# Stick-breaking attention with queries on partitions, VectorE's scan for the running product and weights turned by TensorE

## The chip, the core and the metric

The kernel runs on one core of a Trainium2 chip. The time is device microseconds of one execution. The median of three runs before is 2308.95 us (2308.16 to 2309.34). The profile is one such execution, taken with the hardware profiler.

## What is computed

A trunk of four residual layers (512 tokens, width 1024), each a token mixer and a dense SwiGLU FFN, in float32. Only layer 2 has the mixer that the change touches, stick-breaking attention with 16 heads of 64. Cut to what matters:

```python
def stick_breaking_mixer(h, w_qkv, q_norm, k_norm, w_out):
    qkv = (h @ w_qkv).reshape(b, s, 3, SB_HEADS, SB_HEAD_DIM)
    q, k = rms_norm(qkv[:, :, 0], q_norm), rms_norm(qkv[:, :, 1], k_norm)
    ...
    z = einsum('bhqd,bhkd->bhqk', q_blk, k) * inv_sqrt_d
    mask = key_pos[None, :] < t[:, None]
    log_1m = where(mask, log_sigmoid(-z), 0.0)
    after = cumsum(log_1m, axis=3, reverse=True) - log_1m
    a = where(mask, exp(log_sigmoid(z) + after), 0.0)
    o = einsum('bhqk,bhkd->bhqd', a, v)
    ...
    return o @ w_out
```

A weight is the sigmoid of its own z times the product of the sigmoids of -z of all later keys in front of the query.

## The kernel before

Activations lie as features x tokens. Each big product is made of three of rounded halves (high x high, high x low, low x high): `gemm`, lines 215 to 217. The weights come by SyncE's DMA queue; ScalarE rounds a piece (`wh`, line 108) and VectorE takes the rest (`wl`, line 109), up to four pieces ahead. A scheduler arranges the instructions of each engine when the program is built; which step comes first in the source is set by the string `ATT_STEPS`, and the weights are loaded in the same order.

The steps of the attention are: `pair` (p0 to p7), the projections of q and k for two heads, their normalization (`normal`, with Square, a sum by TensorE, Ln, Exp and Square on ScalarE) and the halves `qq`, `ql`, `kk`; `values` (v0 to v3), v for four heads; `attend` (a0 to a7), two heads; `out` (o0 to o3), the output projection for four heads.

In an `attend` each head has keys on partitions: a tile of z for a block of 128 keys has the queries along the free dimension. Three PSUM tiles hold the causal part of a head, 256, 512 and 512 wide (`z2`, `z13`, `z0`), with a constant -2^100 added to what is masked (`never`, line 867). `softplus` makes log(1 + exp(z)) by Abs, Exp and Ln on ScalarE (lines 873 to 875) and a maximum and sum on VectorE (877); `halves` cuts the result into two rounded parts (881, 882). Since keys lie on partitions, the sum over later keys is a product with a triangle or with a matrix of -1 (`nger`, `none`; `add`, line 910), added into the same PSUM tile as z. An Exp (914) gives the weights, which have the layout that the product with v (842) needs. `split` (220, 221) cuts the output into halves for the output projection.

Of the kernel before, what the change touches and what calls it, by code (L numbers as in the profile page):

```python
# [36 lines left out]
HD = 64  # L37
# [90 lines left out]
def _steps(order, **names):  # L128
    return [(names[s[0]], int(s[1:])) for s in order.split()]
# [7 lines left out]
)  # L137

ATT_STEPS = _steps(
    "p0 v0 p1 a0 p2 v1 p3 a1 a2 p4 v2 o0 a3 p5 a4 v3 p6 o1 a5 p7 a6 a7 o2 o3",  # L140
    p="pair", v="values", a="attend", o="out",
)

SSD_BUFS = dict(u=2, state=3, f=11, a=6, w=6, o=8, c=2, d=5, sel=1)
ATT_BUFS = dict(kk=4, qq=4, ql=4, p=2, v=8, w=3, e=2, a=6, h=6, h2=2, l2=1, o=4)


class Trunk:
# [593 lines left out]
    def attention(self, j, nxt):  # L742
        nc = self.nc
        mm = nc.tensor.matmul
        V = nc.vector
        with self.phase("att", **ATT_BUFS) as tl:
            nge = self.t((P, P))
            nc.gpsimd.memset(nge, -1.0)
            nc.gpsimd.affine_select(
                out=nge, in_=nge, pattern=[[-1, P]], base=0, channel_multiplier=1,  # L750
                compare_op=ALU.is_ge, fill=0.0,
            )
            nger = tl("nger", (P, P), F32R)
            V.tensor_copy(nger, nge)
            none = tl("none", (P, P), F32R)
            V.tensor_scalar(none, self.ones, -1.0, None, op0=ALU.mult)
            V.memset(nge, 0.0)
            V.memset(nge[:HD, :HD], 1.0)
            V.memset(nge[HD:, HD:], 1.0)
            bd = tl("bd", (P, P), F32R)  # L760
            V.tensor_copy(bd, nge)
            qg = tl("qg", (P, 1))
            V.tensor_scalar(qg, self.col("q_norm", 0), 1.0 / math.sqrt(HD), None, op0=ALU.mult)
            kg = self.col("k_norm", 0)
            identb = tl("identb", (P, P), BF16)
            V.tensor_copy(identb, self.ident)
            nc.gpsimd.memset(nge, 0.0)
            nc.gpsimd.affine_select(
                out=nge, in_=nge, pattern=[[1, P]], base=0, channel_multiplier=-1,
                compare_op=ALU.is_gt, fill=-(2.0**100),  # L770
            )
            never = tl("never", (P, P), BF16)
            V.tensor_copy(never, nge)
            rcol = tl("rcol", (P, NB))

            turns = itertools.cycle("mymynmy")

            def bank(shape=(P, SEQ)):
                return self.ps(next(turns), shape)

            def project(q):
                ps = self.ps("g")
# [47 lines left out]
                    heads.append((qq, ql, kk))  # L830
                return heads

            def attend(f, heads, vt):
                po, av = self.ps("s"), []
                for h in range(2):
                    av.append(head(heads[h]))


                at = [(0, 0, 2), (0, 2, 4), (1, 2, 4), (2, 2, 4), (1, 1, 2), (3, 3, 4)]
                for i, (kb, lo, hi) in enumerate(at):  # L840
                    for h in range(2):
                        mm(  # L842
                            po[h * HD : (h + 1) * HD, lo * P : hi * P],
                            vt[kb][:, (2 * f + h) * HD : (2 * f + h + 1) * HD],
                            av[h][kb][:, (lo - kb) * P : (hi - kb) * P],
                            start=i == 0, stop=i == len(at) - 1,
                        )
# [4 lines left out]
            def head(parts):  # L852


                qq, ql, kk = parts

                def zmm(out, *kbs):


                    at = 0  # L860
                    for kb in kbs:
                        n = SEQ - kb * P
                        for i, q in enumerate((qq, ql)):
                            mm(out[:, at : at + n], kk[:, kb * P : (kb + 1) * P],  # L864
                               q[:, kb * P :], start=at == 0 and i == 0, stop=False)
                        at += n
                        mm(out[:, at - n : at - n + P], identb, never, start=False,
                           stop=kb == kbs[-1])

                def softplus(pz):  # L870
                    shape = pz.shape
                    e = tl("e", shape)
                    nc.scalar.activation(e, pz, AF.Abs)
                    nc.scalar.activation(e, e, AF.Exp, scale=-1.0)
                    nc.scalar.activation(e, e, AF.Ln, bias=1.0)
                    w = tl("w", shape)
                    V.scalar_tensor_tensor(w, pz, 0.0, e, op0=ALU.max, op1=ALU.add)
                    return w

                def halves(w, hi, lo):  # L880
                    V.tensor_copy(hi, w)
                    V.tensor_tensor(lo, w, hi.bitcast(F32), op=ALU.subtract)

                def flat(t):
                    return t.rearrange("p b t -> p (b t)")

                z2 = bank((P, 256))
                zmm(z2, 2)  # L890
                w2 = softplus(z2)


                h2, l2 = (tl(t, (P, 3, P), F32R) for t in ("h2", "l2"))
                halves(w2, flat(h2[:, :2]), flat(l2[:, :2]))
                z13 = bank()
                zmm(z13, 1, 3)
                w13 = softplus(z13)
                h13, l13 = tl("h", dt=F32R), tl("h", dt=F32R)
                halves(w13, h13, l13)  # L900
                V.tensor_tensor(w2[:, P:], w2[:, P:], w13[:, 384:], op=ALU.add)
                halves(w2[:, P:], h2[:, 2], l2[:, 2])
                z0 = bank()
                zmm(z0, 0)
                w0 = softplus(z0)
                h0, l0 = tl("h", dt=F32R), tl("h", dt=F32R)
                halves(w0, h0, l0)

                def add(out, left, right, last=False):
                    mm(out, left, right, start=False, stop=last, skip_group_check=True)  # L910

                def weights(z):
                    a = tl("a", z.shape)
                    nc.scalar.activation(a, z, AF.Exp)
                    return a

                both = slice(0, 3, 2)
                add(z2, nger, h2[:, :2])
                add(z2, nger, l2[:, :2])
                add(z2[:, P:], none, h13[:, 384:])  # L920
                add(z2[:, P:], none, l13[:, 384:], True)
                a2 = weights(z2)
                add(z13, nger, h13)
                add(z13, nger, l13)
                add(z13[:, P:384], none, h2[:, both])
                add(z13[:, P:384], none, l2[:, both], True)
                a13 = weights(z13)
                add(z0, nger, h0)
                add(z0, nger, l0)
                for p13, p2 in ((h13, h2), (l13, l2)):  # L930
                    add(z0[:, P:], none, p13[:, :384])
                    add(z0[:, 256:], none, p2[:, both], p2 is l2)
                a0 = weights(z0)
                return a0, a13[:, :384], a2, a13[:, 384:]

            def rstd_columns():

# [201 lines left out]
```

## Time and profile before

| what | us |
|---|---|
| median of three runs | 2308.95 |
| the profiled execution, whole | 2308.4 |
| its span, first to last instruction | 2306.5 |
| attention, first projection to a7's last product with v (1230.9 to 1518.7) | 287.8 |
| PE busy in the whole span | 2284.8 |
| VectorE busy | 1361.4 |
| ScalarE busy | 991.1 |

A matmul's busy time in this profile overlaps that of the next, so a row's mean duration of 0.39 us for a 512 wide matmul is not the time from its start to the start of the next one. The table has the engines' busy time; which wait ends last in a stretch is read from the stretch itself.

### The profile page before, as it was taken

To read this page: it belongs to the slowest core of one execution; us is meant where nothing else is said; L and a number is where in the kernel's file an instruction comes from. 1 tells how busy PE (TensorE), PEld (TensorE's weight loads), DVE (VectorE), ACT (ScalarE), POOL (GpSimd) and SP (SyncE) were. 2 spreads that over 40 slices of the span, in tenths; PEclk is the share of its full clock that TensorE was granted. 3 is DMA by queue.
4 is the path that set the end of the run, shared out by engine and by line. 5 is a ranking of instruction groups with operands and counts; after the bars stand their busy time and mean duration, and the time that the engine had idled before them with its cause. 6 is when DMAs were issued, how large, how long until landed. Compare 5 with 4: busy or idle time off the path is not lost.

```text
span 2306.5 us, 26600 instructions
## 1 busy us (share of the span) xinstructions
PE 2284.8 (99%) x10714; PEld 1857.9 (81%) x10714; DVE 1361.4 (59%) x1946; ACT 991.1 (43%) x1478; POOL 39.7 (2%) x134
## 2 busy tenths in 40 slices
PE   8999999999999999999999999999999999999999
PEld 6788888777877778888888787678888888888887
DVE  9743434778787785444346777874344469534443
ACT  5522323577565764222235766762222244322221
POOL 0000000000000000000000100100000000000000
PEclk9999999999999999999999999999999999999999
DMA  5323322322223222332223221122322223332231
GB/s 161 116 91 100 101 92 76 110 73 74 73 74 92 73 73 92 97 104 91 92 82 101 65 65 55 37 74 95 107 91 92 96 92 95 104 108 92 91 100 64
DMA packets 211898, 205.43 MB, mean 89 GB/s; under 512 B 4800, under 2 KB 204608, under 8 KB 211776
## 3 DMA queue, kind: packets, MB, share of 16 engines
q1 hardware_dynamic: 211632, 203.57, 27.7%
q8 instruction: 84, 1.38, 0.2%
q14 instruction: 38, 0.31, 0.0%
q10 hardware_dynamic: 144, 0.17, 0.0%
HBM read 201.63 MB, written 2.10 MB: 88 GB/s over the span
## 4 chain that ended last, share of the span: by engine, by line
PE 91%; DVE 4%; ACT 3%; DMA 1%; issue 1%; DVEq 0%; ACTq 0%
PE ps L215 28%; PE ps L217 27%; PE ps L216 27%; PE ps L910 2%; PE ps L842 1%; PE ps L673 1%; PE ps L864 1%; PE ps L679 1%; DMA raw<-in_pool_in_dram 1%; ACT wh L108 1%; DVE wl L109 1%; PE ps L642 0%; PE ps L805 0%; PE ps L806 0%; PE ps L804 0%
## 5 line engine op out<-in xcount | busy, mean ns | idle before, releaser
L108 ACT CAST wh<-raw 128x1024 fp32r<-128x1024 f32 (+3 forms) x394 | 402.8, 1023 | 1077.0 <-PE ps L216 838.6
L215 PE MATMUL ps<-xh,wh 128*128 128x512 f32 x2056 | 803.9, 392 | 6.4 <-ACT xh L261 5.9
L217 PE MATMUL ps<-xh,wl 128*128 128x512 f32 x2056 | 803.1, 391 | 0.3 <-DVE wl L109 0.3
L216 PE MATMUL ps<-xl,wh 128*128 128x512 f32 x2056 | 803.0, 391 | 0.3 <-DVE xl L262 0.3
L109 DVE TENSOR_TENSOR wl<-raw,wh 128x1024 fp32r<-128x1024 f32 (+3 forms) x394 | 467.9, 1188 | 77.9 <-ACT wh L108 77.3
L215 PEld LDWEIGHTS ps<-xh,wh 128*128 128x128 f32 x2056 | 385.8, 188 | 89.3 <-ACT xh L261 6.2
L217 PEld LDWEIGHTS ps<-xh,wl 128*128 128x128 f32 x2056 | 385.7, 188 | 83.0 <-issue 2.7
L216 PEld LDWEIGHTS ps<-xl,wh 128*128 128x128 f32 x2056 | 385.7, 188 | 82.0 <-DVE xl L262 1.9
L215 PE MATMUL ps<-h,wh 128*128 128x512 f32 x736 | 286.4, 389 | 0.9 <-DVE x L393 0.9
L216 PE MATMUL ps<-h,wh 128*128 128x512 f32 x736 | 286.3, 389 | 0.0
L217 PE MATMUL ps<-h,wl 128*128 128x512 f32 x736 | 286.3, 389 | 0.0
L343 DVE TENSOR_TENSOR x<-ps,x 128x512 f32<-128x512 f32 x96 | 66.4, 692 | 257.2 <-PE ps L217 257.2
L336 DVE TENSOR_TENSOR g<-ps,g 128x512 f32<-128x512 f32 x88 | 60.6, 691 | 226.3 <-PE ps L217 226.3
L327 DVE TENSOR_TENSOR g<-ps,rstd 128x512 f32<-128x512 f32 x88 | 60.6, 691 | 220.6 <-PE ps L217 220.5
L215 PEld LDWEIGHTS ps<-h,wh 128*128 128x128 f32 x736 | 138.2, 188 | 29.7 <-DVE x L393 1.3
L216 PEld LDWEIGHTS ps<-h,wh 128*128 128x128 f32 x736 | 138.2, 188 | 28.8
L217 PEld LDWEIGHTS ps<-h,wl 128*128 128x128 f32 x736 | 138.2, 188 | 28.8
L215 PE MATMUL ps<-o,wh 128*128 128x512 f32 x192 | 77.2, 405 | 1.2 <-DVE x L736 1.1
L216 PE MATMUL ps<-o,wh 128*128 128x512 f32 x192 | 77.5, 404 | 0.0
L217 PE MATMUL ps<-o,wl 128*128 128x512 f32 x192 | 76.6, 400 | 0.0
L457 DVE SCALAR_TENSOR_TENSOR c<-u,par,c 128x512 f32<-128x512 f32 x96 | 72.0, 750 | 4.1 <-ACT c L452 3.2
L330 DVE TENSOR_TENSOR g<-g,rstd 128x512 f32<-128x512 f32 x88 | 59.9, 685 | 2.6 <-ACT g L329 2.5
(199 smaller groups left out, 2114.0 us busy)
## 6 DMA issues: line engine op xcount, KB each, us to landing
raw<-in_ffn_gate_dram SPq DMA_DIRECT2D x44, 1024.0 KB, 5.1
raw<-in_ffn_up_dram SPq DMA_DIRECT2D x44, 1024.0 KB, 5.2
raw<-in_ffn_down_dram SPq DMA_DIRECT2D x32, 1024.0 KB, 5.1
raw<-in_ssd_in_dram SPq DMA_DIRECT2D x16, 1024.0 KB, 5.2
raw<-in_ffn_down_dram SPq DMA_DIRECT2D x16, 768.0 KB, 4.4
raw<-in_ssd_in_dram SPq DMA_DIRECT2D x16, 512.0 KB, 4.4
raw<-in_ssd_out_dram SPq DMA_DIRECT2D x8, 1024.0 KB, 4.9
raw<-in_sb_qkv_dram SPq DMA_DIRECT2D x16, 512.0 KB, 3.7
```

What stands on the lines that cost most here:

```text
L108: self.nc.scalar.copy(wh, src)
L109: self.nc.vector.tensor_tensor(wl, src, wh.bitcast(F32), op=ALU.subtract)
L215: mm(out, wh, xh, start=start and i == 0, stop=False)
L216: mm(out, wh, xl, start=False, stop=False)
L217: mm(out, wl, xh, start=False, stop=stop and i == n - 1)
L327: nc.vector.tensor_tensor(g, ps, self.rstd, op=ALU.mult)
L330: nc.vector.tensor_tensor(sg, sg, self.rstd, op=ALU.mult)
L336: nc.vector.tensor_tensor(h, ps, h, op=ALU.mult)
L343: nc.vector.tensor_tensor(self.x[d], ps, self.x[d], op=ALU.add)
L457: V.scalar_tensor_tensor(c, u[:, k : k + SEQ], self.col("conv_w", k * nt + ch), c, op0=ALU.mult, op1=ALU.add,)
L673: mm(py[f][i * HD : (i + 1) * HD, bs], xd[b // 2][:, b % 2, 2 * f + i, :], wds[i][:, b], start=True, stop=b == 0,)
L910: mm(out, left, right, start=False, stop=last, skip_group_check=True)
```

## The change

Queries now lie on partitions and keys along the free dimension. A head is done in three `piece`s of 512, 512 and 256 columns (query blocks 0 and 2, then 3, then 1). From z two sigmoids are taken, of -z and of z (lines 846, 847). VectorE's `tensor_tensor_scan` runs backward over each query block's sigmoids of -z (four scans per head, line 851, printed as SCALAR_TENSOR_TENSOR below) and makes the product over later keys; one multiplication per piece (857) gives the weights. TensorE transposes them block by block (875), ten blocks per head, and ScalarE and VectorE in turn copy them out of PSUM (877). The product with v (888) is unchanged in size. z uses the two PSUM banks `m`, the transposes the banks `y` and `n`. Gone are `softplus`, `halves`, the summing products and their two constant matrices. The string of steps is another one: pairs run one further ahead, and o0 to o3 stand elsewhere.

```diff
 ATT_STEPS = _steps(
-    "p0 v0 p1 a0 p2 v1 p3 a1 a2 p4 v2 o0 a3 p5 a4 v3 p6 o1 a5 p7 a6 a7 o2 o3",
+    "p0 p1 v0 a0 p2 v1 a1 p3 a2 v2 p4 a3 o0 p5 v3 a4 p6 a5 p7 a6 o1 a7 o2 o3",
...
-ATT_BUFS = dict(kk=4, qq=4, ql=4, p=2, v=8, w=3, e=2, a=6, h=6, h2=2, l2=1, o=4)
+ATT_BUFS = dict(kk=4, qq=4, ql=4, p=2, v=12, c=2, a=2, e=2, at=3, o=8)
...
+            PIECES = ((0, 2), (3,), (1,))
+            FIRST = {0: 0, 2: 1, 3: 4, 1: 8}
...
+                for qb in qbs:
+                    w = (qb + 1) * P
+                    for q in (qq, ql):
+                        mm(
+                            z[:, at : at + w], q[:, qb * P : (qb + 1) * P], kk[:, :w],
+                            start=at == 0 and q is qq, stop=False,
+                        )
+                    at += w
+                    mm(z[:, at - P : at], identb, never, start=False, stop=qb == qbs[-1])
+                c, a, e = (tl(t, (P, n)) for t in "cae")
+                nc.scalar.activation(c, z, AF.Sigmoid, scale=-1.0)
+                nc.scalar.activation(a, z, AF.Sigmoid)
...
+                    V.tensor_tensor_scan(
+                        back(e, at, w), back(c, at, w), zero.to_broadcast([P, w]), 1.0,
+                        op0=ALU.mult, op1=ALU.add,
+                    )
...
+                V.tensor_tensor(a[:, : n - 1], a[:, : n - 1], e[:, 1:], op=ALU.mult)
...
+            copies = itertools.cycle((nc.scalar.copy, V.tensor_copy))
...
+                for qbs in PIECES:
+                    a = piece(parts, qbs)
+                    n = a.shape[1] // P
+                    pt = self.ps(next(ts), (P, n, P))
+                    for i in range(n):
+                        nc.tensor.transpose(pt[:, i], a[:, i * P : (i + 1) * P], self.ident)
+                    f = FIRST[qbs[0]]
+                    next(copies)(at[:, f : f + n], pt)
...
-                    e = tl("e", shape)
-                    nc.scalar.activation(e, pz, AF.Abs)
-                    nc.scalar.activation(e, e, AF.Exp, scale=-1.0)
-                    nc.scalar.activation(e, e, AF.Ln, bias=1.0)
-                    w = tl("w", shape)
-                    V.scalar_tensor_tensor(w, pz, 0.0, e, op0=ALU.max, op1=ALU.add)
...
-                both = slice(0, 3, 2)
-                add(z2, nger, h2[:, :2])
-                add(z2, nger, l2[:, :2])
```

How the engines' queues change shows in two places. ScalarE, before, where attend a1 begins while the normalization of a pair (232, 233, 235, 789: Ln, Exp, two Squares; 220 a rounding) is under way:

```order
L232 ACTIVATE t_10065<-ps_10058,eps 128x512
L873 ACTIVATE e_10113<-ps_10109 128x256
L233 ACTIVATE t_10065<-t_10065 128x512
L874 ACTIVATE e_10113<-e_10113 128x256
L235 ACTIVATE t_10066<-t_10065 128x512
L789 ACTIVATE t_10073<-p_10025 128x512
L875 ACTIVATE e_10113<-e_10113 128x256
```

No table load stands among these rows; the normalization and the attend alternate.

ScalarE, after, at the corresponding place where a2 begins (846 and 847 are the sigmoids of -z and z, 232, 233 and 235 the normalization):

```order
L232 ACT_TABLE_LOAD
L232 ACTIVATE t_10159<-ps_10152,eps 128x512
L846 ACT_TABLE_LOAD
L846 ACTIVATE c_10211<-ps_10204 128x512
L233 ACT_TABLE_LOAD
L233 ACTIVATE t_10159<-t_10159 128x512
L847 ACT_TABLE_LOAD
L847 ACTIVATE a_10212<-ps_10204 128x512
L235 ACTIVATE t_10160<-t_10159 128x512
```

Before, one table of functions serves all of these; after, a table load stands ahead of each sigmoid that follows a Ln or Exp, and ahead of each Ln or Exp.

TensorE, before, inside a2: z of a head (864), the masking product (867) and the summing products (910) of the same head and the one ahead of it:

```order
L864 MATMUL ps_10364<-qq_9863,kk_9865 128x512
L864 MATMUL ps_10364<-ql_9864,kk_9865 128x512
L910 MATMUL ps_10296<-h_10307,nger_9199 128x512
L910 MATMUL ps_10296<-h_10289,none_9201 128x384
L910 MATMUL ps_10296<-h_10272,none_9201 128x256
L910 MATMUL ps_10296<-h_10290,none_9201 128x384
L910 MATMUL ps_10296<-l_10273,none_9201 128x256
L867 LDWEIGHTS identb_9210
L867 MATMUL ps_10364<-never_9216,identb_9210 128x128
L910 MATMUL ps_10330<-h_10340,nger_9199 128x256
```

The summing products of one piece stand between the products for z of the next.

TensorE, after, inside a2: z (839), the masking product (844), the transposes of finished weights (875) and the first product with v (888); 247 is the second half of a sum for the normalization:

```order
L247 MATMUL ps_10169<-t_10171,bd_9202 128x512
L839 MATMUL ps_10279<-kk_9834,qq_9832 128x512
L839 MATMUL ps_10279<-kk_9834,ql_9833 128x512
L875 MATMUL ps_10236<-ident,a_10230 128x128 x4
L844 LDWEIGHTS identb_9206
L844 MATMUL ps_10279<-never_9213,identb_9206 128x128
L875 MATMUL ps_10253<-ident,a_10247 128x128 x2
L888 MATMUL ps_10202<-at_10203,v_9876 64x256
L839 MATMUL ps_10296<-kk_9834,qq_9832 128x256
```

The bunches of transposes stand where the summing products stood, each behind a sigmoid, a scan and a multiplication of its piece.

## Rows read from the trace of the kernel before

**Rows 1.** The page: shares of the chain that ended last.

```profile
PE 91%; DVE 4%; ACT 3%; DMA 1%; issue 1%; DVEq 0%; ACTq 0%
```

**Rows 2.** Busy time by stretch, cut at the end of each attend (a0 to a7).

```profile
core 0: us, PE busy (x) PEld busy (x) DVE busy (x) ACT busy (x) POOL busy (x), PEclk, DMA share, GB/s
1230.90:1295.00 64.10, 62.95 (x355) 51.78 (x353) 47.14 (x83) 44.57 (x74) 6.85 (x10) 1.00 0.26 76
1295.00:1344.50 49.50, 48.41 (x279) 39.20 (x278) 40.67 (x67) 40.35 (x74) 6.88 (x8) 1.00 0.20 64
1344.50:1358.70 14.20, 14.18 (x98) 11.62 (x98) 7.51 (x18) 7.71 (x15) 0.00 (x0) 1.00 0.19 67
1358.70:1404.70 46.00, 45.13 (x255) 36.07 (x256) 35.91 (x61) 31.58 (x60) 3.21 (x4) 1.00 0.19 58
1404.70:1427.40 22.70, 22.22 (x156) 19.02 (x156) 17.83 (x31) 16.93 (x32) 3.14 (x4) 1.00 0.12 27
1427.40:1477.10 49.70, 48.59 (x241) 37.60 (x240) 37.95 (x64) 31.39 (x58) 3.21 (x4) 1.00 0.25 84
1477.10:1502.20 25.10, 20.74 (x107) 14.42 (x107) 21.58 (x44) 18.12 (x35) 3.08 (x4) 0.93 0.00 0
1502.20:1518.70 16.50, 16.29 (x89) 12.08 (x90) 10.60 (x21) 9.75 (x19) 0.00 (x0) 1.00 0.20 65
```

**Rows 3.** Timeline of PE, layer 1: start, duration, what, shape, count.

```profile
470.30 0.38 PE L606 MATMUL ps<-ident,f 128*128 128x128 f32 x2
470.43 0.48 PE L217 MATMUL ps<-xh,wl 128*128 128x512 f32 x1
470.75 0.39 PE L215 MATMUL ps<-xh,wh 128*128 128x512 f32 x1
470.98 0.40 PE L216 MATMUL ps<-xl,wh 128*128 128x512 f32 x1
```

**Rows 4.** Timeline of PE inside a6, a 256 wide product and the next.

```profile
1477.26 0.28 PE L910 MATMUL ps<-l,nger 128*128 128x256 f32 x1
1477.38 0.33 PE L910 MATMUL ps<-h,none 128*128 128x128 f32 x2
```

**Rows 5.** VectorE's groups, 1230.9 to 1535: shape, count | busy us, mean ns | idle before.

```profile
L877 DVE SCALAR_TENSOR_TENSOR w<-ps,e 128x512 f32<-128x512 f32 (+1 forms) x48 | 28.2, 596 | 2.1 <-ACT e L875 1.6
L882 DVE TENSOR_TENSOR h<-w,h 128x512 fp32r<-128x512 f32 x32 | 22.3, 696 | 0.1
L881 DVE CAST h<-w 128x256 fp32r<-128x256 f32 (+1 forms) x64 | 22.1, 356 | 0.6
L882 DVE TENSOR_TENSOR l<-w,h 128x256 fp32r<-128x256 f32 (+1 forms) x32 | 11.3, 352 | 4.8 <-PE ps L910 4.7
L901 DVE TENSOR_TENSOR w<-w,w 128x128 f32<-128x128 f32 x16 | 5.6, 350 | 0.0
```

**Rows 6.** ScalarE's groups of the same stretch.

```profile
L874 ACT ACTIVATE e<-e 128x512 f32<-128x512 f32 (+1 forms) x48 | 26.5, 560 | 0.5
L875 ACT ACTIVATE e<-e 128x512 f32<-128x512 f32 (+1 forms) x48 | 26.4, 558 | 0.4
L914 ACT ACTIVATE a<-ps 128x512 f32<-128x512 f32 (+1 forms) x48 | 25.2, 525 | 16.9 <-PE ps L910 16.2
L873 ACT ACTIVATE e<-ps 128x512 f32<-128x512 f32 (+1 forms) x48 | 24.5, 519 | 1.9 <-PE ps L867 0.9 <-DVE w L877 0.8
L233 ACT ACTIVATE t<-t 128x512 f32<-128x512 f32 x17 | 10.7, 628 | 0.1
```

**Rows 7.** VectorE's 1024 wide element-wise operation in the same stretch.

```profile
L109 DVE TENSOR_TENSOR wl<-raw,wh 128x1024 fp32r<-128x1024 f32 x32 | 39.5, 1234 | 13.3 <-ACT wh L108 13.3
```

**Rows 8.** Timeline of ScalarE in layer 1, a table load and the next operation.

```profile
638.49 1.28 ACT L461 ACT_TABLE_LOAD   x1
639.79 0.63 ACT L461 ACTIVATE f<-c 128x512 f32<-128x512 f32 x1
```

**Rows 9.** Busy time by stretch, as rows 2, inside a6.

```profile
1490.00:1500.00 10.00, 7.69 (x34) 5.33 (x36) 8.25 (x18) 6.54 (x13) 0.51 (x1) 0.83 0.00 1
```

More of the change, by code (lines that the diff above doesn't have):

```diff
@@ L746, in attention @@
         with self.phase("att", **ATT_BUFS) as tl:
[L747 to L759, printed above, removed]
+            st = self.t((P, P))
+            V.memset(st, 0.0)
+            V.memset(st[:HD, :HD], 1.0)
+            V.memset(st[HD:, HD:], 1.0)
             bd = tl("bd", (P, P), F32R)
-            V.tensor_copy(bd, nge)
+            V.tensor_copy(bd, st)
             qg = tl("qg", (P, 1))
@@ L766, in attention @@
             V.tensor_copy(identb, self.ident)
-            nc.gpsimd.memset(nge, 0.0)
+            st = self.t((P, P))
+            nc.gpsimd.memset(st, 0.0)
             nc.gpsimd.affine_select(
-                out=nge, in_=nge, pattern=[[1, P]], base=0, channel_multiplier=-1,
+                out=st, in_=st, pattern=[[-1, P]], base=0, channel_multiplier=1,
                 compare_op=ALU.is_gt, fill=-(2.0**100),
@@ L772, in attention @@
             never = tl("never", (P, P), BF16)
-            V.tensor_copy(never, nge)
+            V.tensor_copy(never, st)
             rcol = tl("rcol", (P, NB))
-            turns = itertools.cycle("mymynmy")
-            def bank(shape=(P, SEQ)):
-                return self.ps(next(turns), shape)
+            zero = tl("zero", (P, 1))
+            V.memset(zero, 0.0)
+            zs, ts = itertools.cycle("m"), itertools.cycle("yn")
             def project(q):
@@ L831, in pair, with piece @@
                 return heads
-            def attend(f, heads, vt):
[L834 to L840, printed above, removed]
+            PIECES = ((0, 2), (3,), (1,))
+            FIRST = {0: 0, 2: 1, 3: 4, 1: 8}
+            def piece(parts, qbs):
+                qq, ql, kk = parts
+                n = sum(qb + 1 for qb in qbs) * P
+                z = self.ps(next(zs), (P, n))
+                at = 0
+                for qb in qbs:
[10 more added lines that the diff above has]
+                nc.scalar.activation(a, z, AF.Sigmoid)
+                at = 0
+                for qb in qbs:
+                    w = (qb + 1) * P
+                    V.tensor_tensor_scan(
+                        back(e, at, w), back(c, at, w), zero.to_broadcast([P, w]), 1.0,
+                        op0=ALU.mult, op1=ALU.add,
+                    )
+                    at += w
+                V.tensor_tensor(a[:, : n - 1], a[:, : n - 1], e[:, 1:], op=ALU.mult)
+                return a
@@ new lines, in back, with head @@
+            def back(t, at, n):
+                (ps, pn), (s, _) = t.ap
+                return bass.AP(t.tensor, t.offset + s * (at + n - 1), [[ps, pn], [-s, n]])
+            copies = itertools.cycle((nc.scalar.copy, V.tensor_copy))
+            def head(parts):
+                at = tl("at", (P, 10, P))
+                for qbs in PIECES:
[6 more added lines that the diff above has]
+                    next(copies)(at[:, f : f + n], pt)
+                return at
@@ L841, in attend @@
+            def attend(f, heads, vt):
+                po = self.ps("s")
+                ats = [head(heads[h]) for h in range(2)]
+                todo = [(0, 0, 2), (0, 2, 4), (1, 2, 4), (2, 2, 4), (1, 1, 2), (3, 3, 4)]
+                for i, (kb, lo, hi) in enumerate(todo):
+                    b0, b1 = FIRST[lo] + kb, FIRST[hi - 1] + kb
                     for h in range(2):
                         mm(
-                            po[h * HD : (h + 1) * HD, lo * P : hi * P],
+                            po[h * HD : (h + 1) * HD, lo * P : hi * P].rearrange(
+                                "p (b t) -> p b t", t=P
+                            ),
@@ L844, in attend @@
                             vt[kb][:, (2 * f + h) * HD : (2 * f + h + 1) * HD],
-                            av[h][kb][:, (lo - kb) * P : (hi - kb) * P],
-                            start=i == 0, stop=i == len(at) - 1,
+                            ats[h][:, b0 : b1 + 1 : max(b1 - b0, 1)],
+                            start=i == 0, stop=i == len(todo) - 1,
                         )
@@ L850, in attend @@
                 return hi, lo
[L852 to L871, printed above, removed]
-                    e = tl("e", shape)
-                    nc.scalar.activation(e, pz, AF.Abs)
-                    nc.scalar.activation(e, e, AF.Exp, scale=-1.0)
-                    nc.scalar.activation(e, e, AF.Ln, bias=1.0)
-                    w = tl("w", shape)
-                    V.scalar_tensor_tensor(w, pz, 0.0, e, op0=ALU.max, op1=ALU.add)
[L878 to L915, printed above, removed]
-                both = slice(0, 3, 2)
-                add(z2, nger, h2[:, :2])
-                add(z2, nger, l2[:, :2])
[L920 to L934, printed above, removed]
```

## The prediction

> **What bounds the kernel now.** I read the chain of work that ended last first: TensorE holds 91% of it [rows 1]. That is a mean over the program, and the change touches one stage only, so I then cut that stage, 1230.9 to 1518.7 us of the span, at the last product with v of each of the eight attends a0 to a7 [rows 2]. [...] So PE bounds the stage, but by little: in the long a1 stretch (49.5 us) VectorE is busy for 40.67 us and ScalarE for 40.35. "Busy" for PE overlaps from one matmul to the next, so its true load is counted in slots, from start to start: a 128x512 product 0.23 us [rows 3], a 256 wide one 0.12 us [rows 4], 384 and 128 between and below in proportion (0.175 and 0.06, estimates).
>
> **The change, part by part.**
>
> *TensorE.* The 14 summing products per head (line 910) go. Their widths are 4 x 512, 2 x 384, 6 x 256 and 2 x 128: 0.92 + 0.35 + 0.72 + 0.12 = 2.1 us, 34 us over 16 heads. New are 10 transposes per head in three bunches. A bunch of two in the trace takes 0.13 us and delays the next matmul from 0.23 to 0.32 us [rows 3], so 10 x 0.065 + 3 x 0.09 = 0.92 us, 15 us in all. The products for z and with v keep their counts and widths (operands of z trade places; the v product reads two separate blocks of 128, which I price at nothing, at most one extra slot of 0.06 each, 64 x 0.06 = 4 us). Net **-19 us** of PE work; the slots between bunches that also go make it up to -23.
>
> *VectorE.* Lines 877, 881, 882 and 901 go: 28.2 + 22.1 + 22.3 + 11.3 + 5.6 = 89.5 us [rows 5]. New are 48 multiplications (32 of 512 at 0.696, 16 of 256 at about 0.42: 29 us), half of the 48 copies out of PSUM (as line 877's PSUM reads, 24 x 0.596 = 14.3 us [rows 5]) and 64 scans of 128, 384, 512 and 256 per head. No scan runs in this program. From below it costs what an element-wise operation does: 0.696 us at 512 and 1.234 at 1024 [rows 5, 7] give 0.16 fixed and 1.05 ns an element, 1.98 us per head, 31.6 us. From above I take two steps an element, because each result needs the one before it: 3.3 us per head, 53 us. The net is -15 or **+7 us**; I take the dearer end, and keep both for the range. [...]
>
> *ScalarE.* Lines 873, 874, 875 and 914 go: 24.5 + 26.5 + 26.4 + 25.2 = 102.6 us [rows 6]. New are two sigmoids per piece, which read PSUM as line 873 does (2 x 24.5 = 49 us), half the copies (24 x 0.519 = 12.5 us) and table loads. The old functions Abs, Exp and Ln shared one table with the Ln and Exp of the q/k normalization; sigmoid doesn't, and the two kinds of work alternate on ScalarE. The changed program has 40 more loads, none in the first pairs, then 1, 5, 8, 7, 5, 8, 6 and 0 in a0 to a7. In the trace the operation behind a load starts 1.30 us after the load does [rows 8]: 40 x 1.30 = 52 us. Net **+11 us**.
>
> So PE loses about 20 us, and its two partners gain 18. How much reaches the end is read by stretches. I went through each engine's instructions in program order, from one attend's output split to the next, and summed row durations. For a2 on ScalarE: 8 loads 10.4, 12 sigmoids 6.2, 3 copies 1.6, 12 operations of the normalization and the q/k copies at about 0.62 (as [rows 6] line 233 has it) 7.5, one weight cast, two value copies and one split 2.6, together 28.3 us. PE has 20.3 us there.
>
> Counted so, the greatest loads of before are 59.7 (PE), 45.7 (PE; ScalarE 45.0, VectorE 44.1), 16.2, 42.4, 29.2, 45.9, 29.7 and 14.8, 283.6 us over a0 to a7, and the trace has 287.8, so the count can be used. After (PE / VectorE / ScalarE, us):
>
> a0 53.5 / 42.7 / 36.7; a1 27.8 / 27.9 / 29.7; a2 20.3 / 22.8 / 28.2; a3 42.3 / 35.3 / 34.7; a4 30.0 / 31.0 / 30.8; a5 28.2 / 31.5 / 33.4; a6 17.2 / 24.2 / 23.0; a7 8.1 / 15.3 / 8.4.
>
> The greatest sum to 257.6 us, 26 less than before. Three things take from that. Behind a7 the changed order leaves 27.4 us of PE work (the third and fourth output projections) where 21.0 were left: +6.4. Five of the stretches now have two or three engines within 10% of each other. Before there was one such, a1, counted 45.7 us and measured 49.5 [rows 2], 8% over; 8% of the 146 us of a1, a2, a4, a5 and a6 is 12 us. The gaps of the old a6, of which a part stays, are in the count already. And a0 keeps some 4 us of waits, as before (64.1 measured, 59.7 counted); the count's four of 283.6 against 287.8 hold that. So -26 + 6.4 + 12 is -8, and -20 without the 12; I take the middle, nearer the first: **-12 us**.
>
> The rest (the new step order, banks, one constant matrix less) is at nothing: the pairs now run one further ahead, which hides the chain projection, norm, q/k halves behind a whole attend; if that cover fails, an attend starts some 4 us late, in the places where a0 did.
>
> **The rivals.**
> 1. *PE stays the bound throughout.* Scans cost one step an element and the other engines keep ahead: 253.5 for the greatest loads, so -30 + 6.4, **2284 us**. For: PE busy 98% in a1 to a5. Against: ScalarE's loads in a2, a5 are above PE's by 5 to 8 us whatever a scan costs.
> 2. *The gain is swallowed.* ScalarE needs 188 us from a1 to a7, where the stage took 223.7. It must be busy 84% of the time only to break even, since what a0 gains the tail gives back. In a1 before it reached 82% [rows 2]. At 84%: **2308 us**.
> 3. *Slower: ScalarE becomes the bound and waits in order.* Ln, load, sigmoid, load, Exp stand in one queue; a sigmoid whose z is not there holds the norm of the next pair behind it, and a norm whose sums are not there holds sigmoids, and with them scan, transpose and PE. From under 84% on it costs; at 81% a1 to a7 take 232 us, **2316 us**, at 78% 2325. PE, half idle, would lose clock too, as in a6 [rows 9].
> 4. *A table switch costs twice its row.* What decides is how soon the next operation starts; in this trace that is 1.30 us [rows 8], so hardly any chance. At 2.6 us a switch, the 39 loads of a1 to a7 add 51 us to ScalarE's 188, 239 us, which is 15 over before: **2323 us**. [...]
> 5. *The change doesn't do what it says*: a scan that is far slower than two steps; it lands in 3.
>
> **How the numbers follow.** The profiled execution took 2308.4 us (span 2306.5), and the median of the runs is 2308.95, 0.6 above. 2308.4 - 12 is **2296 us**. Chances: the forecast 0.48, rival 1 0.18, rival 2 0.16, rivals 3 and 5 0.15, rival 4 0.03. The lower end is 2282, rival 1 with the -23 of PE; the upper 2314, which takes in rival 2 and the nearer half of 3. Faster by over 0.2% (4.6 us, about what a measurement of this kernel tells from no change): 0.66; within it 0.16; slower 0.18.
>
> **What would show it.** PE's matmul group of line 910 gone, and transposes (line 875) in bunches of 0.3 us. The scan group: 0.7 us at 512 says one step an element, 1.2 two. ScalarE: 40 more loads of 1.28 us, with the operation behind each 1.30 us after. In the stretches a1, a2, a5 and a6, ScalarE busy for 90% and PE waiting for a sigmoid or a scan's product; a wait of PE there on transposes that has VectorE as its end says that VectorE, not ScalarE, binds. The forecast is wrong if a0 to a7 take under 265 or over 285 us, or if the tail behind a7 doesn't grow by some 6 us.

## The result, and the profile after

The changed kernel takes **2328.28 us** (2327.25 to 2330.09), the kernel before 2308.71 beside it: a ratio of 1.0086, interval 1.0068 to 1.0103. It is 0.9% slower, where 2296 was forecast with 2314 as the upper end. The profiled execution has a span of 2325.5 us, 19.0 more than before.

The page of after, the shares of the chain that ended last, to set against [rows 1]:

```profile
PE 87%; ACT 5%; DVE 5%; issue 1%; DMA 1%; SPq 0%; POOL 0%; DVEq 0%; ACTq 0%; POOLq 0%
```

TensorE has lost four points of the chain; its two partners have gained three. The stage, cut after, as [rows 2] before, at each attend's last product with v (columns as there):

```profile
1230.90:1290.95 60.05, 57.48 (x320) 45.33 (x318) 45.91 (x73) 40.27 (x65) 6.40 (x8) 1.00 0.25 75
1290.95:1326.85 35.90, 32.32 (x204) 26.12 (x204) 25.96 (x36) 28.28 (x43) 2.45 (x4) 0.95 0.15 47
1326.85:1363.57 36.72, 28.16 (x158) 22.33 (x158) 22.08 (x31) 26.69 (x39) 3.43 (x4) 0.81 0.04 13
1363.57:1410.80 47.23, 44.89 (x235) 35.06 (x235) 32.45 (x45) 33.02 (x47) 3.24 (x4) 1.00 0.19 56
1410.80:1449.80 39.00, 34.55 (x215) 27.92 (x214) 29.75 (x40) 29.01 (x44) 3.97 (x4) 0.96 0.31 97
1449.80:1486.90 37.10, 32.31 (x165) 23.07 (x165) 27.65 (x40) 31.45 (x46) 3.96 (x4) 1.00 0.11 38
1486.90:1513.20 26.30, 21.53 (x106) 15.04 (x107) 22.36 (x35) 21.78 (x31) 2.81 (x4) 0.94 0.03 7
1513.20:1529.30 16.10, 12.28 (x73) 8.01 (x72) 14.13 (x23) 7.81 (x16) 0.00 (x0) 0.89 0.19 64
sum 298.40, PE 263.53 PEld 202.87 DVE 220.28 ACT 218.31 POOL 26.26; mean PE 32.94 PEld 25.36 DVE 27.54 ACT 27.29 POOL 3.28
```

The stage takes 298.4 us, 10.6 more than the 287.8 of [rows 2], and what follows a7 takes 796.2 (2325.5 - 1529.3) in place of 787.8, 8.4 more; together the 19.0 of the span. In the stage PE's busy time fell from 278.5 (the sum of [rows 2]) to 263.5, 15.0 less, while its idle time rose from 9.3 to 34.9, 25.6 more. **PE did lose work, and stood idle for longer than the work it lost.** No engine is full: VectorE is busy for 74% of the stage, ScalarE for 73, and in a2, which has the granted clock at 0.81, PE for 77, VectorE for 60 and ScalarE for 73.

What PE waited for, the longest of the waits of PE alone over 1230.9 to 1530 (engine, line <- engine and line waited for: us in total, times, longest). Before:

```profile
PE ps L910 <- DVE h L881: 3.3, 6, 0.7
PE ps L215 <- DVE x L736: 1.1, 2, 0.9
```

After:

```profile
PE ps L875 <- DVE a L857: 10.1, 12, 2.2
PE ps L839 <- ACT a L847: 8.8, 8, 2.7
PE ps L888 <- DVE t L236: 3.8, 2, 2.9
```

The transposes (875) wait for VectorE's multiplication, which stands behind the scan; the next z (839) waits for the second sigmoid (847) of an earlier piece, which frees its PSUM bank.

The groups that the terms of the forecast rest on, 1230.9 to 1560 after, by shape (count | busy us, mean ns | idle before). VectorE, to set against [rows 5]; the profile prints the scan of line 851 as TENSOR_TENSOR_SCAN:

```profile
L851 DVE TENSOR_TENSOR_SCAN e<-c,zero 128x512 f32<-128x512 f32 x16 | 19.4, 1214 | 0.0
L851 DVE TENSOR_TENSOR_SCAN e<-c,zero 128x384 f32<-128x384 f32 x16 | 14.9, 932 | 0.0
L851 DVE TENSOR_TENSOR_SCAN e<-c,zero 128x256 f32<-128x256 f32 x16 | 11.7, 734 | 0.0
L851 DVE TENSOR_TENSOR_SCAN e<-c,zero 128x128 f32<-128x128 f32 x16 | 6.7, 421 | 8.0 <-ACT c L846 7.9
L857 DVE TENSOR_TENSOR a<-a,e 128x511 f32<-128x511 f32 x32 | 21.5, 682 | 5.6 <-ACT a L847 5.2
```

ScalarE, to set against [rows 6, 8]:

```profile
L847 ACT ACTIVATE a<-ps 128x512 f32<-128x512 f32 x32 | 19.4, 605 | 0.6 <-PE ps L875 0.5
L232 ACT ACT_TABLE_LOAD x12 | 15.4, 1283 | 0.2
L233 ACT ACT_TABLE_LOAD x12 | 15.4, 1283 | 0.2
L846 ACT ACT_TABLE_LOAD x10 | 12.8, 1283 | 0.2
L847 ACT ACT_TABLE_LOAD x6 | 7.7, 1283 | 0.1
```

The scans sum to 52.7 us (53 in the forecast, the dearer end) and there are 40 loads, 51.3 us. So the durations were priced right. How they act on PE is seen inside a2. Timeline of ScalarE (start, duration, what; in brackets idle time before it):

```profile
1344.52 1.28 ACT L232 ACT_TABLE_LOAD   x1
1345.81 0.69 ACT L232 ACTIVATE t<-ps,eps 128x512 f32<-128x512 f32 x1
1346.52 1.28 ACT L846 ACT_TABLE_LOAD   x1
1347.81 0.60 ACT L846 ACTIVATE c<-ps 128x512 f32<-128x512 f32 x1
1348.42 1.28 ACT L233 ACT_TABLE_LOAD   x1
1349.72 0.63 ACT L233 ACTIVATE t<-t 128x512 f32<-128x512 f32 x1
1350.26 0.35 ACT L877 COPY at<-ps 128x256 f32<-128x256 f32 x1
1350.51 0.63 ACT L235 ACTIVATE t<-t 128x512 f32<-128x512 f32 x1
1351.15 1.28 ACT L847 ACT_TABLE_LOAD   x1
1352.45 0.60 ACT L847 ACTIVATE a<-ps 128x512 f32<-128x512 f32 x1
```

VectorE at the same place (rows between these are left out):

```profile
1344.27 2.12 DVE L818 TENSOR_TENSOR ql<-p,qq 64x512 fp32r<-64x512 f32 x2
1347.12 0.95 DVE L851 TENSOR_TENSOR_SCAN e<-c,zero 128x256 f32<-128x256 f32 x1
1348.11 0.42 DVE L857 TENSOR_TENSOR a<-a,e 128x255 f32<-128x255 f32 x1
1351.17 0.69 DVE L236 SCALAR_TENSOR_TENSOR t<-ps,t 128x512 f32<-128x512 f32 x1 [1.46 <-ACT t L235]
1353.29 0.68 DVE L857 TENSOR_TENSOR a<-a,e 128x511 f32<-128x511 f32 x1
1353.89 1.22 DVE L851 TENSOR_TENSOR_SCAN e<-c,zero 128x512 f32<-128x512 f32 x1
```

TensorE (rows between these are left out):

```profile
1348.59 0.44 PE L875 MATMUL ps<-ident,a 128*128 128x128 f32 x2 [2.17 <-DVE a L857]
1351.91 1.11 PE L888 MATMUL ps<-at,v 128*64 128x256 f32 x2 [2.89 <-DVE t L236]
1354.12 1.09 PE L875 MATMUL ps<-ident,a 128*128 128x128 f32 x4
```

Between the two sigmoids of one piece (1347.81 and 1352.45) stand two loads, two operations of the next pair's normalization (233, 235) and a copy of turned weights (877). VectorE idles 1.46 us for Square (235) and multiplies (1353.29) only when the second sigmoid is there; PE idles 2.89 us, since its product with v waits for line 236, which stands behind Square. PE's 2.17 us before that have another origin: from 1344.27 on VectorE is busy almost without a gap, with two subtractions for `ql`, a copy (877), a scan and the multiplication that the transposes wait for. So each of the partners holds PE once here. The product with v waits for line 236 since the sums of the normalization and the outputs of the attends share one PSUM bank. The granted clock is lower too; busy time of two stretches of 10 us in a2:

```profile
1340.00:1350.00 10.00, 5.43 (x21) 3.40 (x21) 9.57 (x14) 9.53 (x15) 3.43 (x4) 0.82 0.01 2
1350.00:1360.00 10.00, 7.16 (x28) 5.71 (x28) 7.56 (x11) 6.60 (x13) 0.00 (x0) 0.50 0.00 0
```

In the stretch in which PE is busy for 5.43 of 10 us the granted clock has a mean of 0.82, in the next it is 0.50, half of full speed, and the four transposes at 1354.12 take 1.09 us, where four at 1340.10 take 0.66. In the stage its mean is 0.95 (1.00 in all stretches of before but a6, [rows 2]).

### The profile page after: what moved, and what is told of

Same layout as the page of the kernel before. It is cut to its first block, busy times and chain, and to the rows that moved or that the text cites. A ratio compares the mean times of both kernels' runs of the same rounds, so it can differ in the third digit from the quotient of the medians.

```text
span 2325.5 us, 26443 instructions
## 1 busy us (share of the span) xinstructions
PE 2279.9 (98%) x10650; PEld 1849.0 (80%) x10650; DVE 1368.6 (59%) x1889; ACT 1011.4 (43%) x1446; POOL 39.6 (2%) x132
## 4 chain that ended last, share of the span: by engine, by line
PE 87%; ACT 5%; DVE 5%; issue 1%; DMA 1%; SPq 0%; POOL 0%; DVEq 0%; ACTq 0%; POOLq 0%
PE ps L215 27%; PE ps L216 27%; PE ps L217 27%; PE ps L673 1%; PE ps L888 1%; DVE e L851 1%; DVE wl L109 1%; ACT L233 1%; ACT wh L108 1%; PE ps L679 1%; ACT L232 1%; PE ps L875 0%; PE ps L642 0%; DVE a L857 0%; DMA raw<-in_pool_in_dram 0%
```

## Experiments

Theories. **S**: VectorE's scans hold PE. **L**: ScalarE's table loads do. **B**: PSUM banks. **O**: the new order of steps. **C**: the loss is TensorE's clock. Ratios are to the kernel before.

### Loads, scan, and both

*e1_noload* (Exp has a table that the normalization uses too, and its trace has none of the 40 loads; it leaves out the sigmoid, the durations of the ACTIVATEs stay; the build orders the queues anew, TensorE's in some 50 places):

```diff
-                nc.scalar.activation(c, z, AF.Sigmoid, scale=-1.0)
-                nc.scalar.activation(a, z, AF.Sigmoid)
+                nc.scalar.activation(c, z, AF.Exp, scale=-1e-38)
+                nc.scalar.activation(a, z, AF.Exp, scale=1e-38)
```

> Both sigmoids are replaced by Exp of z times a scale of 1e-38, so that the weights are all near one: the output is not the reference's. The number, width and operands of ScalarE's passes stay, and the 40 table loads inside attention go (93 loads in the program become 53). The order of the queues shifts a little, since the build places work around the loads. Theory L (table loads in ScalarE's queue hold sigmoids and the next pair's norm, and PE behind them): ScalarE has 52 us less, attention shrinks by 25 us or more, under 2303 us in all, and the granted clock stays at full speed. Theory S (VectorE's scans take two steps an element and VectorE binds): at most 8 us less, 2320 or above. Theory B (z has only two PSUM banks, and PE waits for the second sigmoid of the piece before): some 5 us less, about 2323.

Measured: 2311.72 us (2309.89 to 2312.68), 1.001 (1.000 to 1.0019): 16.6 below after. None of the three expectations holds: it lies between L's 2303 and S's 2320.

*e2_scan1* (an addition of the same width, 687 ns at 512 columns where the scan takes 1214; it leaves out the running product; the order on all three engines is the same):

```diff
-                    V.tensor_tensor_scan(
-                        back(e, at, w), back(c, at, w), zero.to_broadcast([P, w]), 1.0,
-                        op0=ALU.mult, op1=ALU.add,
+                    V.tensor_tensor(
+                        back(e, at, w), back(c, at, w), zero.to_broadcast([P, w]),
+                        op=ALU.add,
                     )
```

> Each scan is replaced by an element-wise addition of the same operands and width, one step an element; the running product is left out, so the output is not the reference's. The order of all queues is that of the changed kernel. It takes 0.53 us from a 512 wide scan, 21 us of VectorE over 16 heads. Theory L: VectorE is rarely what ends a wait, 2328 minus 3 to 7, about 2323. Theory S: 15 us or more, 2313 or below. Theory B: under 3 us, 2326.

Measured: 2314.85 us, 1.0022 (1.0013 to 1.0032): 13.4 below after, 2 us short of what S expected and far from L and B.

*e3_both* has both edits.

> The two edits of the runs before together: no table loads in attention and no scans (output not the reference's). What is left is the changed kernel's PE work with light partners. Theory L: within 6 us of the run without loads alone. Theory S: within 6 us of the run without scans alone. If each holds PE in turn: clearly below both, 2280 to 2290, as the rival of the prediction in which PE stays the bound. Theory B: both removed and still above 2315.

Measured: 2295.55 us, 0.9938 (0.9923 to 0.9952): 32.7 below after and 13.9 below the kernel before. That is clearly below both single runs, as expected if each holds PE in turn, but above the 2280 to 2290 given for it. Its stage, cut from 1230.9 to a7's last product with v, and that of after cut in the same way:

```profile
1230.90:1494.05 263.15, 248.99 (x1458) 197.73 (x1456) 199.59 (x316) 162.73 (x290) 27.68 (x32) 0.98 0.19 59
```

```profile
1230.90:1529.35 298.45, 263.58 (x1468) 202.91 (x1466) 220.28 (x321) 218.31 (x331) 26.26 (x32) 0.95 0.17 53
```

The two effects add, 16.6 + 13.4 = 30.0 against 32.7 for both. 51.3 us of loads cost 16.6, a third of their length; the 21.0 us by which the scans are longer than the additions (52.7 against 31.7) cost 13.4, two thirds. Each edit takes away its own wait. PE's waits in e1, then in e2:

```profile
PE ps L875 <- DVE a L857: 12.3, 19, 2.1
PE ps L839 <- ACT a L847: 2.7, 4, 0.8
```

```profile
PE ps L839 <- ACT a L847: 8.3, 7, 2.7
PE ps L875 <- DVE a L857: 7.4, 7, 2.9
```

Without loads the next z waits 2.7 us for line 847 in place of 8.8; with the short scan the transposes wait 7.4 for line 857 in place of 10.1. So neither S nor L holds alone: each piece goes through a chain ScalarE, VectorE, PE, and work on either partner lies on PE's path.

The scan's price is the cleaner of the two, since after and e2, and e1 and e3 (16.2 apart), run the same sequence on all three engines. Where the loads go, the order changes too; that an order changed in as many places need not move the time is seen in e4 below.

Between after and e3 the stage is 35.3 us shorter. PE runs the same instructions in both programs, ten of them (some 2 us) behind a7 in e3 and in the stage in after, yet is busy 263.58 and 248.99 us: up to 14.6 us of the difference is PE slower at the same work, 20.7 its idle time. "Busy" holds slots at a lower granted clock (0.50 over 1350 to 1360 in after) and, in front of gaps, the end of a matmul that no other covers (0.39 us busy for a slot of 0.23, [rows 3]); the trace doesn't part these two.

### Banks and step order

*e4_bank3* gives z three banks and the transposes two in place of three:

```diff
-            zs, ts = itertools.cycle("m"), itertools.cycle("yn")
+            zs, ts = itertools.cycle("mmn"), itertools.cycle("y")
```

> Nothing is left out. The PSUM tiles of z take three banks in turn (m, m, n) in place of two, the transposes two (y) in place of three. Theory B: PE's waits for the sigmoid of z (20.7 us in the changed kernel) go, 10 us or more less, 2318 or below. Theories L and S: the sigmoid comes late because ScalarE is late, so a third bank moves the wait elsewhere: 2328 within 4 us.

Measured: 2328.57 us, 1.0082. Nothing, as L and S expected. PE's wait for line 847 is down to 0.5 us from 8.8, but the transposes wait 13.6 for line 857 in place of 10.1, and z waits 6.6 for v (line 800) on ScalarE. (The expectation's 20.7 us adds to PE's 8.8 the 11.9 of its weight loads, which wait at the same time.)

*e5_oldsteps* is the changed kernel with the old string of steps:

```diff
-    "p0 p1 v0 a0 p2 v1 a1 p3 a2 v2 p4 a3 o0 p5 v3 a4 p6 a5 p7 a6 o1 a7 o2 o3",
+    "p0 v0 p1 a0 p2 v1 p3 a1 a2 p4 v2 o0 a3 p5 a4 v3 p6 o1 a5 p7 a6 a7 o2 o3",
```

> The changed kernel with the step order of the kernel before (the string only); nothing is left out. Theory O (the new order, which leaves the output projections o2 and o3 whole behind a7 and costs 8.4 us there, is a part of the loss): the tail behind a7 shrinks by some 6 us and the time to about 2321. Theory L and S (loads and scans each hold PE, whatever the order): what the tail gives back a6 and a7 take, which then stand together with less PE work beside them: 2328 or above.

Measured: 2329.31 us, 1.0086 (1.0071 to 1.0101). Nothing, again as L and S expected. Its stage ends at 1536.2 in place of 1529.3: PE work goes from the tail back into the stage, and the whole stays as it is. B and O fall.

### Grouping the loads

*e6_grouped* holds each pair's Ln and Exp behind the last sigmoid so far and the next sigmoids behind that Exp, and loads one table that has both Ln and Exp; its trace has 13 loads (7 ahead of sigmoids, 6 ahead of Ln), not the 15 of the expectation, where after has 40:

```diff
+                with behind("sig"):
+                    if gain is qg:
+                        nc.scalar.preload_act_table_set("natural_log_exp_and_others")
+                    r = self.rsqrt(None, pss, HD, load=False)
+                pins["exp"] = self.exp
...
+                with behind("exp"):
+                    nc.scalar.activation(c, z, AF.Sigmoid, scale=-1.0)
+                    pins["sig"] = nc.scalar.activation(a, z, AF.Sigmoid).ins
```

> The changed kernel with ScalarE's order pinned: each pair's Ln and Exp stand together behind the last sigmoid of an attend, the next attend's sigmoids behind them, and one table that holds Ln and Exp is loaded for both. 15 loads in attention instead of 40; nothing else is changed. If a load costs its share of what the run without loads gained (17 us for 40, 0.42 each): 25 fewer give 10 us, about 2318. If only the alternation inside a chain (sigmoid, Ln, sigmoid, Exp) costs: nearly all of the 17, about 2312. If the pins hold up the next pair as much as the loads did: 2328 or above.

Measured: 2316.05 us, 1.0029 (1.0019 to 1.0039): 12.2 below after, for 27 loads or 34.6 us less of ScalarE, between the 10 and the 17 of the expectations. That is 0.35 of their length, near the third of e1.

*e7_grouped_diff* builds on e6 and leaves out the second sigmoid: the sigmoid of z times the product over later keys is that product less the one that has its own key too, so a weight is a difference of neighbours of the scan.

```diff
-                V.tensor_tensor(a[:, : n - 1], a[:, : n - 1], e[:, 1:], op=ALU.mult)
+                for qb in qbs:
+                    w = (qb + 1) * P
+                    nc.gpsimd.memset(a[:, at + w - 1 : at + w], 0.0)
+                    V.tensor_tensor(
+                        a[:, at : at + w - 1], e[:, at + 1 : at + w], e[:, at : at + w - 1],
+                        op=ALU.subtract,
+                    )
+                    at += w
```

> As the grouped run, and the weights are made as a difference of neighbouring running products, so that the second sigmoid goes: ScalarE loses 24.5 us more, VectorE keeps its work (a subtraction per query block in place of a multiplication per piece). Theory S (with the loads mostly gone VectorE is what PE waits for, as the run without loads shows 12 us of waits for its product): at most 5 us under the grouped run. Theory L (ScalarE still holds PE): 10 us or more under it.

Measured: 2312.08 us (2311.05 to 2315.91), 1.0014 (1.0004 to 1.0023): 4 below e6, as S expected. The second sigmoids were 25.7 us of ScalarE, so here only 0.15 of ScalarE's time came back (VectorE has 64 subtractions for 48 multiplications, 2.7 us more).

*e8_grouped_diff_light* puts all copies of turned weights on ScalarE and the subtraction for `kk` on GpSimd:

```diff
-                    V.tensor_tensor(kk[other], k[own], kk[own].bitcast(F32), op=ALU.subtract)
+                    nc.gpsimd.tensor_tensor(kk[other], k[own], kk[own].bitcast(F32), op=ALU.subtract)
...
-            copies = itertools.cycle((nc.scalar.copy, V.tensor_copy))
+            copies = itertools.cycle((nc.scalar.copy,))
```

> As the run before, and VectorE is relieved: all copies of the transposed weights go to ScalarE (14 us) and the subtraction for kk to GpSimd (11 us). That is about the 21 us that the run without scans took from it. Theory S: 10 to 13 us under the run before, near 2300, under the kernel before. If GpSimd's subtraction delays the pairs, or ScalarE's copies the chain: no gain over the run before.

Measured: 2316.13 us, 1.003: 4 worse than e7, though VectorE has less to do; the expectation without a gain holds. Timelines of e8 in a2, GpSimd and VectorE:

```profile
1342.84 3.19 POOL L831 TENSOR_TENSOR kk<-p,kk 64x512 fp32r<-64x512 f32 x2 [2.12 <-ACT kk L830]
```

```profile
1343.15 1.29 DVE L871 TENSOR_TENSOR a<-e 128x127 f32<-128x127 f32 x1
1344.83 2.29 DVE L861 TENSOR_TENSOR_SCAN e<-c,zero 128x512 f32<-128x512 f32 x1
```

The same two operations of VectorE in e7, where GpSimd does not subtract:

```profile
1311.98 0.27 DVE L871 TENSOR_TENSOR a<-e 128x127 f32<-128x127 f32 x1
1317.69 1.22 DVE L861 TENSOR_TENSOR_SCAN e<-c,zero 128x512 f32<-128x512 f32 x1
```

While GpSimd subtracts (1342.84 to 1346.03), VectorE's operations last longer: 1.29 us in place of 0.27 and 2.29 in place of 1.22. Beside GpSimd's subtractions from 1274.99 and from 1460.46 a scan of 512 takes 2.30 us. So here the time was not taken off VectorE, and GpSimd's subtraction takes 1.53 us in the mean where VectorE's took 0.69. e11, below, has the same copies without it.

### What is left above the kernel before

*e9_fill* adds two products to the changed kernel in front of each bunch of transposes, whose result nobody reads, to keep PE at work in its gaps. They take a PSUM bank from the transposes, which in e4 cost nothing:

```diff
-            zs, ts = itertools.cycle("m"), itertools.cycle("yn")
+            zs, ts = itertools.cycle("m"), itertools.cycle("y")
...
+                self.hot = c
...
+                    warm = self.ps("n", (P, n * P))
+                    for _ in range(2):
+                        mm(warm, identb, self.hot.bitcast(BF16)[:, 1::2], start=True, stop=True)
```

> The changed kernel with two products of 512 columns ahead of each of the 48 bunches of transposes, whose result nobody reads (some 48 x 2 x 0.21 = 20 us more of PE work, in the place where PE waits for the scan's product). If the loss is TensorE's granted clock (0.994 over the span against 0.999 before, and 0.50 in some stretches of 10 us of a2): the clock comes back to 0.998 or more, and the time falls below 2328, to 2318 to 2326, in spite of the work. If the loss is the chain sigmoid, scan, transpose itself and the clock only follows: the fill lies in idle time for the greater part, the clock comes back, and the time stays at 2325 to 2335. If PE's slots are what binds: +20, some 2348.

Measured: 2339.34 us, 1.013 (1.0115 to 1.0145): 11.1 above after, granted clock over the span 0.994 to 0.996, after's 0.991 to 0.994. None of the three expectations holds: of its 19 us (an estimate: 64 slots of 0.23 and 32 of 0.12, [rows 3, 4]) more than half lie on the path, and the clock is hardly better. In part the fill waits itself, for the first sigmoid (7 us of idle time ahead of it).

*e12_grouped_fill* is the same on e7.

> The variant with grouped loads and one sigmoid (2312; granted clock 0.97 in the stage) with the same two idle products of 512 columns ahead of each bunch of transposes. If TensorE's clock is what is left above the kernel before: the clock of the stage comes back to 0.99 or more and the time is 2302 to 2309. If not, the fill's 20 us now meet a PE that has less idle time (273.6 of 298 us busy): 2316 to 2330.

Measured: 2323.78 us, 1.0064 (1.0049 to 1.0079): 11.7 above e7, in the range expected if the clock is not what is left. The profiled executions have a clock of 0.97 in e7's stage and of 0.99 in e12's, but e7's is 2.7 us above its median, and over the span seven of e7's ten have 0.998, as e12 has. So the two runs don't give the clock's own share; they show only that time can't be bought back in this way.

*e10_grouped_scan1* is e7 with the addition in place of the scan (diff as in e2; it leaves out the running product).

> The variant with grouped loads and one sigmoid (2312) with the scan taken by an element-wise addition of the same width, which takes one step an element and not two (leaves out the running product). If VectorE's scan lies on the chain by itself, as the 13 us of the same edit on the changed kernel say: 2312 - 13 = 2299, some 10 below the kernel before. If the scan cost only because ScalarE's loads had used up the slack: 2312 - 0 to 4 = 2308 to 2312.

Measured: 2297.13 us, 0.995 (0.9933 to 0.9966): 15.0 below e7 for 20.7 us less of VectorE, the order on all three engines the same, and near the 2299 expected if the scan lies on the chain by itself. The stage of e10, then of e7 (an execution 2.7 us above e7's median):

```profile
1230.90:1502.89 271.99, 257.27 (x1491) 202.71 (x1489) 203.53 (x343) 164.16 (x257) 30.86 (x98) 0.99 0.19 59
```

```profile
1230.90:1520.41 289.51, 265.04 (x1490) 204.79 (x1489) 222.49 (x343) 165.78 (x257) 31.08 (x98) 0.97 0.18 55
```

In e7 VectorE is busy for 77% of the stage and ScalarE for 57, and still 72% of the scan's extra time reaches the end. So the scan costs by itself, not because the loads had used up its slack.

*e11_grouped_copies* is e7 with all 48 copies on ScalarE.

```diff
-            copies = itertools.cycle((nc.scalar.copy, V.tensor_copy))
+            copies = itertools.cycle((nc.scalar.copy,))
```

> The variant with grouped loads and one sigmoid (2312) with all 48 copies of turned weights out of PSUM on ScalarE, and none on VectorE: VectorE loses 24 x about 0.55 = 13 us, ScalarE (busy 170 of 298 us there) gains 24 x 0.5 = 12. If VectorE's load is what binds: two thirds of 13, as for the scan, so 2303, below the kernel before. If it is the length of the chain and not an engine's load: 2310 to 2314. The run with the GpSimd subtraction (2316) had the same copies; if it was the copies that cost there and not GpSimd's 1.53 us: 2316.

Measured: 2309.39 us (2308.70 to 2311.55), 1.0003 (0.9993 to 1.0012): 2.7 below e7, level with the kernel before, and 6.7 below e8, which is what GpSimd's subtraction cost there. It lies 0.6 under the 2310 to 2314 expected if the length of the chain counts, and 6 above the 2303 of a share of VectorE's load. By the shares above, 14 us off VectorE at two thirds give 9.4, and 12 on ScalarE at a third take 4 back: 5, twice the 2.7. So the shares don't carry over from one edit to another. This is the fastest of the versions that do the whole computation in the new way; none beats the kernel before.

## The prediction, step by step

- *PE bounds the kernel before*: right, as [rows 2] show: PE is busy for 98 to 100% of seven of the eight stretches, and in a6 for 20.74 of 25.1 us.
- *TensorE, -19 to -23 us*: right in size. With light partners (e3, the same PE instructions) PE is busy for 2266.2 us of the span, 18.6 less than the 2284.8 before; in the stage 249.0, 29.5 less, of which 9.7 is the longer tail behind a7 (797.5 and 787.8).
- *VectorE, +7, two steps an element*: right. The scan of 512 takes 1214 ns, as priced from 0.696 at one step, and VectorE's busy time over the span rose by 7.2 (1361.4 to 1368.6); rival 1, which needed one step, fell with it. From 128 to 512 columns the scans take 2.07 ns an element (421 and 1214 ns), the additions of e2 in their place 1.04 (289 and 687 ns).
- *ScalarE, +11, 40 loads of 1.30*: right in the durations, 114.9 us new for the 102.6 that went, but not in the time that the engine is held: its busy time over the span rose by 20.3 (991.1 to 1011.4). A pass overlaps the next by some 0.1 us (1349.72 + 0.63, and the copy starts at 1350.26), so the 192 passes that went held it for less than their sum, and a load overlaps nothing (1345.81 + 0.69, and the load starts at 1346.52). The operation behind a load starts 1.29 to 1.30 us after it (1346.52 to 1347.81, 1348.42 to 1349.72). Rival 4 fell: no run shows its 2.6 us a switch, which was the author's assumption; in its place the next ACTIVATE starts 10 to 20 ns behind the load's end.
- *Tail, +6.4*: 8.4. e5 shows that this is no loss: with the old order it goes back into the stage and the time stays.
- *The sum of the greatest loads, and 12 us for balanced stretches*: **this is the step that failed.** It counted 257.6 us; the stage took 298.4, 40.8 more, where the 12 and 4 of waits in a0 were allowed. The five stretches priced at 8% over their greatest load are 28.5 us over their 146.5 (a1 35.9 for 29.7, a2 36.7 for 28.2, a4 39.0 for 31.0, a5 37.1 for 33.4, a6 26.3 for 24.2), 20%. One of them, a2, has no two engines within 10% by the count itself (20.3, 22.8, 28.2), and it is the furthest off. a0 (60.1 for 53.5) and a3 (47.2 for 42.3), where PE was still the greatest, are 11.5 over; for them nothing but the old 4 was allowed. Taking the greatest assumes that the other engines run beside it. By it, the count's own numbers without the loads (1.30 each, 1, 5, 8, 7, 5, 8, 6 of them) give 9 less, and e1 gave 16.6; with scans 2.6 us shorter in each attend 4 less, and e2 gave 13.4. The runs showed in its place that the partners' time adds to PE's path before either is full: 16.6 us by the loads and 13.4 by the scan's second step (e1 to e3). The count held for before, where PE's idle time is 9.3 of 287.8 us; that a shorter PE would find the same cover was assumed. The one stretch of before in which PE was short of work spoke against it: in a6 PE is idle for 4.4 of 25.1 us, with VectorE busy for 86% and ScalarE for 72 [rows 2].
- *Forecast wrong over 285 us for the stage*: 298.4, so by its own mark it was.
- *Rival 3*, ScalarE waiting in order, is what happened as far as ScalarE goes, in the place it named: Ln, load, sigmoid, load, Exp, at the price of 2316 to 2325: a1 to a7 took 238.4 us, between its 232 and 241 (188 of ScalarE at 81 and at 78%). The whole lies above its 2325, since a0 gave 4 us (64.1 to 60.05) and the tail took 8.4, where the two were to cancel. Two things in it were off. ScalarE did not become the bound (the trace has it busy for 178.0 us, 75% of a1 to a7, where 188 were counted); it cost as a link of the chain. And VectorE's scan, which no rival named as a cost in itself, is nearly as dear (13.4 to 16.2). "PE, half idle, would lose clock too" came true, 0.50 in 1350 to 1360.
- *Banks and order at nothing*: right (e4, e5).

**What stays open**: why e7 and e11, with partners busy for 57 to 77% of the stage, only reach the kernel before. Their PE still waits on line 871 (9.0 and 9.3 us) and on the first sigmoid (8.1 and 7.4), so a longer chain per piece is likely, but no run shortened it with the work on all engines kept. Two places of the chain were not tried: the first sigmoid itself waits 7.9 and 7.4 us for a scan, whose input tile `c` has two buffers, and the sums of the normalization share their one PSUM bank with the products with v (3.8 us of PE's waits in after). The clock's own share is open too. An estimate of its bound, if the lower clock is the 0.50 of 1350 to 1360: a mean of 0.95 over 298.4 us is some 30 us at 0.50, in which at most 15 us of PE work at full clock are lost, and 0.98 over the 263.15 of e3 some 5, so at most some 10 of the 35.3 us between after and e3.

## To carry to other kernels

Before summing "the greatest load of each stretch", ask whether the engines' work is independent there: where one piece goes through three engines in turn, and the bound engine has little other work to put into the gaps, price the partners' added time as a share on the path, and not at nothing until they are full. Here the share was a third of the loads' and two thirds or more of the scan's, but other edits had other shares (e7, e11), so it is a range and not a constant. Ask of a function that needs another table how it interleaves with the neighbours on that queue: grouping the uses took 40 loads to 13 and gave back 12 us. When work leaves the bound engine and its partners grow by as much, the change has spent its gain.

## What the runs showed of the hardware

Beside GpSimd's subtractions of two SBUF tensors VectorE's operations lasted longer: a scan took 2.29 us in place of 1.22, and a subtraction of 127 columns 1.29 in place of 0.27 (e8 and e7). GpSimd's two took 3.19 us from 1342.84 on; VectorE's subtraction began 0.31 us after their start, and the scan ended 1.09 us after their end. Over the attention the 16 scans of 512 have a mean of 1550 ns in e8 and 1217 in e7, the 16 subtractions of 127 columns 456 and 270.

The price of a partner's time was not the same for both, nor from edit to edit. A microsecond of ScalarE cost 0.32 (e1), 0.35 (e6) and 0.15 (e6 to e7), one of VectorE 0.64 (e2), 0.77 (e1 to e3) and 0.72 (e10), though both were busy for nearly the same share of the stage in after (73 and 74%). These are prices of this chain of work, not of the engines.
